# The later steps of the mLSTM gates at later places among the projections' matmuls, and the masked factors as a step of their own

## The chip, the cores and the metric

The kernel runs on one core of a Trainium2 chip. The metric is the device time of one execution in microseconds (us). The engines of the core are named as in the profile: PE is the matrix engine (PEld its weight loads), DVE the vector engine, ACT the scalar engine with the activation functions, POOL the GpSimd engine, SP the engine that here issues nearly all DMAs (its queue is shown as SPq). Each engine works through its own instructions in order and waits at an instruction until what it needs is there.

## The reference, cut to what matters

One encoder layer over 2048 rows of 1024 columns, in float32. After an RMS norm with conditioning, one input projection gives the columns of a windowed attention and of a bidirectional mLSTM with 4 heads, among them 16 gate columns. The mLSTM needs a depthwise convolution over time of its query and key columns, and from the gates a handful of small vectors per chunk of 128 rows:

```python
logf = blocks(jax.nn.log_sigmoid(f_pre))
bcum = jnp.cumsum(logf, axis=-1)
a = b_last[..., None] - bcum + ig
a_max = jnp.max(a, axis=-1)
w = jnp.exp(a - a_max[..., None])
...
m_new = jnp.maximum(bl + m_st, am)      # scan over the 16 chunks
decay = jnp.exp(bl + m_st - m_new)
...
m_t = jnp.maximum(g, jnp.max(dlog, axis=-1))
dw = jnp.exp(dlog - m_t[..., None])
inter = jnp.exp(g - m_t)
```

This is done for 4 heads, 2 directions and 16 chunks, 128 rows of 128 numbers in all. Then follow the chunks' products, the attention, an output projection and a SwiGLU feed-forward part with 2816 columns.

## The kernel before, in words

Float32 products are made from three matmuls of rounded halves (high by high, high by low, low by high), each of 128x128 weights and 512 columns. The order of the work is written out by hand on PE throughout. In the stretch that matters here it is written out for DVE, ACT, POOL and SP as well (`manual_schedule`): each engine's program order is the order in which the Python code issues its instructions. In some other parts (the end of the first part, the attention part, the end of the feed-forward part) a planner orders the engines other than PE.

The stretch is the loop over 252 steps `i` that starts the projections of the mLSTM's keys and queries. In each step it calls `pull(1)`, which issues one more matmul of the projection now being filled in (`proj_mm`, line 497) and then `beat()`, which counts down the entries of a list of postponed actions (`put_soon`) and runs those that are due. Before the matmul of step `i`, two generators are run on: `gates()` (the gates' arithmetic) and `w_out_ops()` (products of the output projection's weights with a gate row, and their sums, on POOL, with their DMAs on SP). A `yield 62` in one of them means: what follows is issued in step 62, ahead of the matmul of that step.

```python
for i in range(2 * 96 + 60):
    for j, g in enumerate(steps):
        while due[j] <= i:
            due[j] = next(g)
    ...
    pull(1)
```

A projection tile of 128 columns has four blocks of 512 rows, 24 matmuls each (`conv_tile`): block 0 takes steps 0 to 23, block 1 steps 24 to 47, and so on; the next tile starts at step 96, the third at 192. The blocks' sums stand in two PSUM banks in turn, so the matmuls of a block wait until the block before the last one has been read out. In the step after a block's last matmul, ACT takes the middle tap out of the bank (line 524) and the two edge columns (525, then 527 and 528). Seven beats later DVE adds the two outer taps, also out of the bank (`sides`, lines 511 and 512). Then tanh on ACT, a product on DVE and a store to `qk_d` on SP follow one after another for the block before (`finish`; all three are shown as line 121). For the first tile this gives, on DVE: sides of block 0 at the end of step 30, of block 1 at 54, of block 2 at 78, of block 3 at 102; the products of blocks 0 to 3 at the ends of steps 61, 85, 109 and 115; the tanhs on ACT at 57, 81, 105 and 111; the stores on SP at 66, 90, 114 and 120.

`gates()` goes through these parts: the log-sigmoid and its running sums (up to line 869), constants for picking rows (871 to 874), at step 52 the running maximum and the last column of each chunk (`st`, 881 and 882), then a small matmul (885, `rps`) that brings the chunks' values into rows, the scan over the chunks on DVE (887 to 892, `sr`, `mn`, `rw`), an exp (894), the masked factors `rx` (897), four small matmuls that bring the results back to columns (899 and 900, `cps`: the first pair from `rw`, the second from `rx`), their use (`mc`, `dec`, `ux`: 903 to 909), three exps and three products (911 to 917), four stores of rows to `bc_d` on SP (920, 921), three transposes on PE (924) and their copies (926). The mLSTM reads these results from step 252 on; its first scan (over the chunks backwards) transposes key blocks (611, `ktp`) that come back from `qk_d` by DMA (588, `mqk`).

`w_out_ops()` works through eight units. Unit n has its POOL products and sums (957, 959, 970) at steps 33, 36 and 41 plus 24n, its stores (972, 973) at 49 + 24n and (962) at 62 + 24n, and issues the loads of unit n + 1 (935) at 41 + 24n; units 4 to 7 stand 10 steps further back.

Of the kernel before, what the change touches and what calls it, by code (L numbers as in the profile page):

```python
# [36 lines left out]
def hybrid_layer_kernel(  # L37
# [14 lines left out]
    def bank(tag, name):  # L52
        return pp.tile([P, 512], F32, tag=tag, name=name, bufs={"g": 2, "a": 2, "b": 1, "c": 2, "d": 1}[tag])
# [782 lines left out]
    def gates():  # L836
# [43 lines left out]
        for sl, j in ((lo_, 127), (hi_, 0)):  # L880
            dve.tensor_scalar(st[sl, 0], spot[sl], b[sl, j:j + 1], None, MUL)
            dve.scalar_tensor_tensor(st[sl, 1], spot[sl], cm[sl, j:j + 1], st[sl, 0], MUL, ADD)
        yield 62
        ps = bank("c", "rps")
        pe.matmul(ps[:8, :2 * NT], pick, st.rearrange("p j c -> p (j c)"), start=True, stop=True)
        sr = s2.tile([8, 2, NT], F32, name="sr", bufs=1)
# [3 lines left out]
        dve.tensor_copy(rw[:, 0, 1:], mn[:, :-1])  # L890
        dve.tensor_tensor(rw[:, 1], sr[:, 0], mn, SUB)
        dve.tensor_tensor(rw[:, 2], rw[:, 1], rw[:, 0], ADD)
        yield 76
        act.activation(rw[:, 2], rw[:, 2], AF.Exp)
        yield 84
        rx = s2.tile([8, 8, NT], F32, name="rx", bufs=1)
        dve.tensor_tensor(rx, rowm, rw[:, 2].unsqueeze(1).to_broadcast([8, 8, NT]), MUL)
        ps = bank("c", "cps")
        pe.matmul(ps[:, :2 * NT], rowm.rearrange("q r c -> q (r c)"), rw[:, :2].rearrange("q j c -> q (j c)"), start=True, stop=True)
        pe.matmul(ps[:, P:2 * P], ones[:8, :], rx.rearrange("q r c -> q (r c)"), start=True, stop=True)  # L900
# [6 lines left out]
        act.activation(q4(dec[:, 64:])[:, :, ::-1], q4(ps[:, P + 64:2 * P]), AF.Copy)  # L907
        ux, it, em, wr = gt("gux"), gt("git"), gt("gem"), gt("gwr")
        dve.tensor_scalar(ux, cm, mc[:, 0:1], None, MAX)
        yield 92  # L910
        act.activation(it, ux, AF.Exp, bias=mc[:, 0:1], scale=-1.0)
        act.activation(wr, r, AF.Exp, bias=mc[:, 1:2])
        dve.tensor_tensor(em, b, ux, ADD)
        yield 100
        act.activation(em, em, AF.Exp, scale=-1.0)
        dve.tensor_scalar(it, it, float(128 ** -0.5), None, MUL)
        dve.tensor_scalar(ux, ux, -1.0, None, MUL)
        yield 112
        for d, sl in ((0, lo_), (1, hi_)):
            sp.dma_start(bc_d[:, :, d, :].rearrange("h c t -> (h c) t"), ux[sl])  # L920
            sp.dma_start(bc_d[:, :, 2 + d, :].rearrange("h c t -> (h c) t"), it[sl])
# [58 lines left out]
    w_second = proj_cols(C_QM)  # L980
    win = ExitStack()
    steps = [gates(), w_out_ops()]
    due = [0, next(steps[1])]
    win.enter_context(tc.manual_schedule(engines={getattr(mybir.EngineType, e) for e in ("DVE", "Activation", "Pool", "SP")}))
# [1024 lines left out]
```

## Time and profile before

| | us |
|---|---|
| median of 3 runs | 2263.84 (2262.03 to 2265.5) |
| the profiled execution, its own time | 2262.92 |
| span of the profile (first to last instruction) | 2261.1 |
| PE busy in the span | 2219.7 (98%) |
| DVE busy | 1611.6 (71%) |
| ACT busy | 1061.4 (47%) |
| POOL busy | 1041.5 (46%) |

The gates' stretch runs from 175.4 us (the first transposes of the gates) to 238.4 us (the first transpose of the mLSTM). Times in the rows of the timeline are microseconds from the start of the span; a row's second number is its duration, a bracket at its end says how long the engine stood idle before it and who ended that.

### The profile page before, as it was taken

Reading aid. Unit: us, or ns where it says so; the run is one execution under the profiler, and the core shown is the slowest. Engines: PE = TensorE matmul, PEld = TensorE weight load, DVE = VectorE, ACT = ScalarE, POOL = GpSimd, SP = SyncE. Lnnn points to the kernel's source line nnn. Section 1 sums busy time; section 2 is a strip of 40 time slices with the busy share of each in tenths; the row PEclk is TensorE's granted clock in tenths of the full one; section 3 lists DMA queues with packets and bytes.
Section 4 is the critical chain, followed back from the end, with each engine's and each line's share of the span. In section 5 each row is a group of like instructions: output and inputs, shape, how many; then the busy total and the mean of one; then the engine's idle time right before and its main releaser. Section 6 shows DMA issues by size and latency. Waiting matters only on the chain.

```text
span 2261.1 us, 32357 instructions
## 1 busy us (share of the span) xinstructions
PE 2219.7 (98%) x10818; PEld 1858.9 (82%) x10818; DVE 1611.6 (71%) x2942; ACT 1061.4 (47%) x2209; POOL 1041.5 (46%) x904
## 2 busy tenths in 40 slices
PE   7999999999999999999999999999999999999998
PEld 4997888888788878888888888888888888888887
DVE  6776667656688887886667777777766665785694
ACT  5433665554678746354445444433333333233452
POOL 1016535334344333436666565467665663692020
PEclk8999999999999999999999999999999999999999
DMA  8566755685766576764343455534333374543462
GB/s 323 169 208 200 227 166 170 190 241 168 209 185 189 175 242 209 266 234 156 107 144 110 153 182 170 170 126 140 98 112 98 112 260 141 172 149 95 145 217 93
DMA packets 337063, 391.28 MB, mean 173 GB/s; under 512 B 20874, under 2 KB 234234, under 8 KB 336896
## 3 DMA queue, kind: packets, MB, share of 16 engines
q1 hardware_dynamic: 335616, 388.65, 52.8%
q8 instruction: 85, 1.39, 0.3%
q14 instruction: 82, 0.67, 0.1%
q10 hardware_dynamic: 1280, 0.56, 0.1%
HBM read 269.95 MB, written 119.19 MB: 172 GB/s over the span
## 4 chain that ended last, share of the span: by engine, by line
PE 88%; DVE 5%; ACT 2%; DMA 2%; issue 1%; POOL 1%; SPq 0%; POOLq 0%; ACTq 0%; DVEq 0%
PE gps L497 15%; PE fp L56 12%; PE fp L57 12%; PE fp L58 12%; PE fo L58 5%; PE fo L57 5%; PE fo L56 5%; PE ops L56 2%; PE ops L58 2%; PE ops L57 2%; PE atp L807 1%; PE num L708 1%; PE kvp L621 1%; PE num L710 1%; PE pv L56 1%
## 5 line engine op out<-in xcount | busy, mean ns | idle before, releaser
L497 PE MATMUL gps<-hT,whi 128*128 128x512 f32 x1088 | 395.1, 418 | 0.0
L58 PE MATMUL fo<-w,al 128*128 128x512 f32 x616 | 239.8, 389 | 0.0
L56 PE MATMUL fo<-w,ah 128*128 128x512 f32 x616 | 239.7, 389 | 0.0
L57 PE MATMUL fo<-w,ah 128*128 128x512 f32 x616 | 239.7, 389 | 0.0
L497 PE MATMUL gps<-hT,wlo 128*128 128x512 f32 x544 | 226.1, 416 | 0.0
L497 PEld LDWEIGHTS gps<-hT,whi 128*128 128x128 f32 x1088 | 199.5, 189 | 23.5
L56 PE MATMUL fp<-T,S 128*128 128x512 f32 x528 | 206.7, 391 | 0.3 <-ACT s L1622 0.3
L57 PE MATMUL fp<-T,S 128*128 128x512 f32 x528 | 205.7, 389 | 0.0
L58 PE MATMUL fp<-T,S 128*128 128x512 f32 x528 | 205.4, 389 | 0.0
L1763 DVE TENSOR_TENSOR al<-al,ah 128x1024 fp32r<-128x1024 f32 x77 | 115.0, 1499 | 106.9 <-ACT ah L1762 106.7
L1762 ACT ACTIVATE ah<-al 128x1024 fp32r<-128x1024 f32 x77 | 81.7, 1060 | 181.5 <-DMA al<-a_d 175.9
L1465 DVE TENSOR_TENSOR S<-sf,S 128x512 fp32r<-128x512 f32 x86 | 126.9, 1513 | 37.1 <-ACT S L1464 36.9
L1465 DVE TENSOR_TENSOR A<-graw,A 128x512 fp32r<-128x512 f32 x86 | 128.9, 1518 | 16.7 <-ACT A L1464 16.6
L58 PE MATMUL fp<-B,A 128*128 128x512 f32 x352 | 136.9, 389 | 0.0
L56 PE MATMUL fp<-B,A 128*128 128x512 f32 x352 | 136.9, 389 | 0.0
L57 PE MATMUL fp<-B,A 128*128 128x512 f32 x352 | 136.9, 389 | 0.0
L58 PEld LDWEIGHTS fo<-w,al 128*128 128x128 f32 x616 | 115.6, 188 | 24.6 <-DVE al L1763 0.5
L56 PEld LDWEIGHTS fo<-w,ah 128*128 128x128 f32 x616 | 115.6, 188 | 24.1
L57 PEld LDWEIGHTS fo<-w,ah 128*128 128x128 f32 x616 | 115.6, 188 | 24.1
L800 POOL TENSOR_SCALAR ap<-ap,adn 128x384 f32<-128x384 f32 (+1 forms) x124 | 70.2, 585 | 132.2 <-PE atp L807 62.2
L1469 POOL TENSOR_TENSOR sf<-A,A22r 128x512 f32<-128x512 f32 x42 | 59.3, 1412 | 151.0 <-DMA A22r<-in_w_ffn_in_dram 134.5
L1632 DVE SCALAR_TENSOR_TENSOR g<-t,g 128x512 f32<-128x512 f32 x44 | 42.1, 957 | 114.0 <-ACT t L1631 114.0
(440 smaller groups left out, 6156.9 us busy)
## 6 DMA issues: line engine op xcount, KB each, us to landing
al<-a_d SPq DMA_DIRECT2D x77, 512.0 KB, 4.2
wmod<-in_w_mod_dram SPq DMA_DIRECT2D x48, 512.0 KB, 7.4
graw<-in_w_ffn_in_dram SPq DMA_DIRECT2D x43, 512.0 KB, 3.8
a_d<-ka SPq DMA_DIRECT2D x66, 256.0 KB, 4.9
bc<-bc_d SPq DMA_DIRECT2D x64, 256.0 KB, 4.8
hop_d<-n SPq DMA_DIRECT2D x56, 256.0 KB, 4.1
a_d<-u SPq DMA_DIRECT2D x55, 256.0 KB, 4.6
mqk<-qk_d SPq DMA_DIRECT2D x44, 256.0 KB, 4.5
```

Source lines behind the costliest of these rows:

```text
L56: pe.matmul(o, lh, rh, start=first, stop=False, skip_group_check=skip)
L57: pe.matmul(o, lh, rl, start=False, stop=False, skip_group_check=skip)
L58: pe.matmul(o, ll, rh, start=False, stop=last, skip_group_check=skip)
L497: pe.matmul(ps, w[i == 2][:, k, :], hT[n](i == 1, k), start=(k == 0 and i == 0), stop=(k == KT - 1 and i == 2))
L621: pe.matmul(kvp[:, :129], kn, vw, start=True, stop=True)
L708: pe.matmul(num[:, d, :129], sc[:, d, :], va_c, start=True, stop=st is None)
L800: pool.tensor_scalar(p, p, dn[:, g:g + 1], 0.0, MUL, ADD)
L1465: dve.tensor_tensor(t[:, 1, :], f, t[:, 0, :].bitcast(F32), SUB)
L1469: add.tensor_tensor(f1, a21, a22, ADD)
L1632: dve.scalar_tensor_tensor(g0, t0, 1.0, g0, ADD, MUL)
L1762: act.activation(ah, al.bitcast(F32), AF.Copy)
L1763: dve.tensor_tensor(al, al.bitcast(F32), ah.bitcast(F32), SUB)
```

## The change

Only the step numbers in `gates()` change, from the small matmul `rps` on, and one `yield` is added between the masked factors `rx` and the matmuls `cps`. What stood at step 62 (`rps` and the scan) stands at 74, the exp goes from 76 to 86, `rx` from 84 to 92, `cps` and what uses it from 84 to 102, the exps from 92 to 110 and from 100 to 118, the stores, transposes and copies from 112 to 130.

```diff
             dve.scalar_tensor_tensor(st[sl, 1], spot[sl], cm[sl, j:j + 1], st[sl, 0], MUL, ADD)
-        yield 62
+        yield 74
         ps = bank("c", "rps")
         pe.matmul(ps[:8, :2 * NT], pick, st.rearrange("p j c -> p (j c)"), start=True, stop=True)
...
         dve.tensor_tensor(rw[:, 2], rw[:, 1], rw[:, 0], ADD)
-        yield 76
+        yield 86
         act.activation(rw[:, 2], rw[:, 2], AF.Exp)
-        yield 84
+        yield 92
         rx = s2.tile([8, 8, NT], F32, name="rx", bufs=1)
         dve.tensor_tensor(rx, rowm, rw[:, 2].unsqueeze(1).to_broadcast([8, 8, NT]), MUL)
+        yield 102
         ps = bank("c", "cps")
         pe.matmul(ps[:, :2 * NT], rowm.rearrange("q r c -> q (r c)"), rw[:, :2].rearrange("q j c -> q (j c)"), start=True, stop=True)
         pe.matmul(ps[:, P:2 * P], ones[:8, :], rx.rearrange("q r c -> q (r c)"), start=True, stop=True)
...
         dve.tensor_scalar(ux, cm, mc[:, 0:1], None, MAX)
-        yield 92
+        yield 110
         act.activation(it, ux, AF.Exp, bias=mc[:, 0:1], scale=-1.0)
         act.activation(wr, r, AF.Exp, bias=mc[:, 1:2])
         dve.tensor_tensor(em, b, ux, ADD)
-        yield 100
+        yield 118
         act.activation(em, em, AF.Exp, scale=-1.0)
         dve.tensor_scalar(it, it, float(128 ** -0.5), None, MUL)
         dve.tensor_scalar(ux, ux, -1.0, None, MUL)
-        yield 112
+        yield 130
         for d, sl in ((0, lo_), (1, hi_)):
             sp.dma_start(bc_d[:, :, d, :].rearrange("h c t -> (h c) t"), ux[sl])
             sp.dma_start(bc_d[:, :, 2 + d, :].rearrange("h c t -> (h c) t"), it[sl])
```

## The prediction

> **What bounds the kernel now.** I read the page's busy times first, then PE's waits between 140 and 280 us, then the stretch's table and the timelines of PE, DVE, POOL, ACT and SP around the moved steps.
>
> ```profile
> PE 2219.7 (98%) x10818; PEld 1858.9 (82%) x10818; DVE 1611.6 (71%) x2942; ACT 1061.4 (47%) x2209; POOL 1041.5 (46%) x904
> PE cps L900 <- DVE rx L897: 2.1, 1, 2.1
> PE rps L885 <- DVE st L882: 1.7, 1, 1.7
> 190.00:200.00 10.00, 6.40 (x29) 4.91 (x30) 9.04 (x14) 2.44 (x7) 9.84 (x12) 1.00 0.77 242
> 206.80 31.77 PE gps L497 x140
> ```
>
> PE is the bound of the kernel. Between 140 and 280 us it waits twice only, at the two small gate matmuls that the change moves. In the table's row for 190 to 200 us PE works 6.40 of 10 us, DVE 9.04 and POOL 9.84, at a granted clock of 1.00: here the vector engine sets the pace. The last row, of the chain of work, gives the price of one step: 31.77 / 140 = 0.227 us.
>
> ```profile
> 189.24 0.61 PE L497 MATMUL gps<-hT,whi 128*128 128x512 f32 x2
> 191.52 0.23 PE L885 MATMUL rps<-st,pick 128*8 128x32 f32 x2 [1.66 <-DVE st L882]
> 191.68 0.50 PE L497 MATMUL gps<-hT,wlo 128*128 128x512 f32 x1
> 192.02 0.64 PE L497 MATMUL gps<-hT,whi 128*128 128x512 f32 x2
> 196.93 0.40 PE L899 MATMUL cps<-rw,rowm 8*128 8x32 f32 x2
> 199.41 0.48 PE L900 MATMUL cps<-rx,ones_r 8*128 8x128 f32 x2 [2.08 <-DVE rx L897]
> 199.82 0.73 PE L497 MATMUL gps<-hT,whi 128*128 128x512 f32 x2
> 241.62 0.27 PE L611 MATMUL ktp<-ident,mqk 128*128 128x128 f32 x1
> ```
>
> The matmuls at 189.24 are those of steps 60 and 61. Step 62 was due at 189.24 + 2 x 0.227 = 189.69, and `rps` started at 191.52: 1.83 us lost. The second pair of `cps` was due one pair after 196.93 (the `rps` pair took 191.68 - 191.52 = 0.16), at 197.09 to 197.33 if the pair's whole 0.40 is counted, and started at 199.41: 2.1 to 2.3 us lost, I take 2.2. Together 4.03 us, 0.18% of the time. This is all that the change can save.
>
> **The change part by part.** Nothing is added or removed but one place to stop; only positions move. What counts is which work stands ahead of which on each queue, and what is late next.
>
> ```profile
> 190.28 1.19 DVE L882 SCALAR_TENSOR_TENSOR st<-spot,gates,st 64x16 f32<-64x16 f32 x1
> 191.50 0.75 DVE L511 SCALAR_TENSOR_TENSOR cacc<-gps,cvw,cacc 128x511 f32<-128x511 f32 x1
> 192.35 0.75 DVE L512 SCALAR_TENSOR_TENSOR cacc<-gps,cvw,cacc 128x511 f32<-128x511 f32 x1
> 193.02 1.04 DVE L121 SCALAR_TENSOR_TENSOR cacc<-ctanh,cacc 128x512 f32<-128x512 f32 x1
> 193.98 0.17 DVE L887 COPY sr<-rps 8x32 f32<-8x32 f32 x1
> 194.74 1.19 DVE L890 COPY rw<-mn 8x15 f32<-8x15 f32 x1
> 195.85 0.15 DVE L891 TENSOR_TENSOR rw<-sr,mn 8x16 f32<-8x16 f32 x1
> 196.04 1.15 DVE L892 TENSOR_TENSOR rw<-rw 8x16 f32<-8x16 f32 x1
> 197.95 0.75 DVE L512 SCALAR_TENSOR_TENSOR cacc<-gps,cvw,cacc 128x511 f32<-128x511 f32 x1
> 198.62 0.73 DVE L897 TENSOR_TENSOR rx<-rowm,rw 8x128 f32<-8x128 f32 x1
> 200.15 1.23 DVE L909 TENSOR_SCALAR gates<-gates,mc 128x128 f32<-128x128 f32 x1
> 201.30 1.80 DVE L121 SCALAR_TENSOR_TENSOR cacc<-ctanh,cacc 128x512 f32<-128x512 f32 x1
> ```
>
> *`rps`, 62 to 74.* `st` is there at 191.47 as before, since nothing ahead of it moves; PE follows a DVE result after 0.05 us (191.47 to 191.52). Without the old wait PE runs on to step 72, due at 189.24 + 12 x 0.227 = 191.96. There block 3 of the tile takes the bank of block 1, and DVE reads that bank (lines 511 and 512, queued behind `st`) until 193.10. So PE stops at step 72 until 193.15: **a new wait of 1.19 us**. Before, PE came to step 72 only at 192.02 + 9 x 0.227 = 194.06, and the bank was free. `rps` at step 74 then starts at 193.15 + 0.45 = 193.60 and is through by 193.9. DVE is busy with line 121 until 194.06, so `sr` starts at its old time and the scan ends as before, at 197.19. The side sums of block 2 (issued at step 78 in both versions) end at 198.70 as before.
>
> *Step 96, a second bank.* `rps` and its restart cost 192.02 - 191.52 - 0.227 = 0.27. Step 96 (next tile, bank of block 2) is due at 193.60 + 0.27 + 22 x 0.227 = 198.86; DVE frees the bank at 198.70. No wait, with 0.1 us to spare; a miss of a few tenths here would cost as much.
>
> *The exp, 76 to 86, and the exps after it.* They now stand behind other tanhs. The three rows of ACT show what that costs:
>
> ```profile
> 188.28 1.28 ACT L121 ACT_TABLE_LOAD   x1
> 197.22 0.21 ACT L894 ACTIVATE rw<-rw 8x16 f32<-8x16 f32 x1 [1.37 <-DVE rw L892]
> 197.34 0.61 ACT L121 ACTIVATE ctanh<-cacc 128x512 f32<-128x512 f32 x1
> ```
>
> The first tanh (step 57) brought its table at 188.28; exp at 197.22 and tanh at 197.34 follow each other with no load between. All moved exps stand behind step 57 in both versions: no load is added, cost 0. The exp still starts at about 197.2, when the scan is done, and tanh of block 1, now ahead of it, has finished by then.
>
> *`rx`, 84 to 92, and `cps`, 84 to 102.* Here the order on DVE turns over: the product of block 1 (line 121, step 85) now stands **ahead of `rx`** instead of behind `ux`. POOL decides what it costs.
>
> ```profile
> 192.76 1.90 POOL L970 TENSOR_TENSOR ts<-by,ts 128x256 f32<-128x256 f32 x2
> 194.62 1.28 POOL L957 TENSOR_TENSOR bx<-bx,gb 128x512 f32<-128x512 f32 x1
> 195.86 1.30 POOL L959 TENSOR_TENSOR by<-by,gb 128x512 f32<-128x512 f32 x1
> 198.50 1.52 POOL L970 TENSOR_TENSOR ts<-by,ts 128x256 f32<-128x256 f32 x2
> ```
>
> The 8x15 copy `rw` took 1.19 us and ended at 195.93, just after POOL's product (194.62 + 1.28 = 195.90); `rw` at 196.04 ended with POOL's next one; between two POOL instructions the same kind took 0.15. I therefore let each such DVE instruction end behind the POOL instruction that it meets. The product of block 1 starts behind 198.70, meets the first sum of the row at 198.50 (half of 1.52) and takes 1.04 us like its twin at 193.02, to about 199.8; `rx` then meets the second sum and takes 0.73, to 200.55. PE sees it at 200.60. The first pair of `cps` is due at 198.86 + 6 x 0.227 = 200.22, the second at 200.38: **a wait of 0.2 us**. Bounds: with DVE undisturbed (the product for what is left of 1.80 when POOL's 1.30 is taken off, and 0.15), `rx` is ready at 199.4 and the wait is 0. With the dearest rows (1.80 and 1.23) it is ready at 201.73 and the wait 1.4. I take 0.2 since the POOL row that it meets is known.
>
> The Trainium skill (SBUF — State Buffer, § Who interferes with whom) says that of a GpSimd instruction and a VectorE one that needs the shared pair of ports, the later waits for the whole of the other, and that this does not hold for VectorE instructions with one SBUF input and no two-port mode. The trace agrees: lines 511 and 512, which read PSUM, stay at 0.75 us while POOL works. This speaks against the change, for it lets `rx` meet a second POOL instruction; by the rule the saving is the sum below, and without it 0.2 us more.
>
> *Steps 110 to 130.* After `rx` the rest of DVE's work up to step 130 is the same as before in another order. The bank of block 3, wanted at step 120, is read out behind `mc` and `ux` (1.23): `cps` restarts PE at about 201.0, DVE ends the side sums at 201.2 + 1.23 + 1.6 = 204.0, step 120 comes at 201.1 + 18 x 0.227 = 205.2: no wait, 1.2 us to spare. If that cover is gone it costs PE that much less the margin. The transposes at step 130 need `em`, whose exp comes some 2 us earlier on ACT; step 252 reads the copies 27 us later. Cost 0.
>
> *The four stores to `bc_d`, 112 to 130, on SP.*
>
> ```profile
> 203.13 0.34 SPq L121 DMA_DIRECT2D qk_d<-cacc  x1
> 206.32 0.51 SPq L920 DMA_DIRECT2D bc_d<-gates  x1
> 208.31 0.60 SPq L921 DMA_DIRECT2D bc_d<-gates  x1
> 208.95 0.60 SPq L935 DMA_DIRECT2D bx<-in_w_out_dram  x1
> 230.02 0.63 SPq L972 DMA_DIRECT2D wo_d<-bx  x1
> 235.83 0.33 SPq L588 DMA_DIRECT2D mqk<-qk_d  x1
> ```
>
> They are moved past the loads of unit 4 (935, step 113), the stores of blocks 2 and 3 (114, 120) and those of unit 3 (121), which all go 208.95 - 206.32 = 2.6 us earlier in the queue, and they now stand in front of the stores at 144 and the loads at 147. The queue also stops less: the store of block 1 waited for its product until 203.13; that product now ends at 199.8. So SP is some 3 us early at step 113 and, with DVE done with step 118 at about 207.5, about 3 us early again behind the four stores. POOL gets unit 4 earlier by as much. Cost 0, as long as that holds (a rival below).
>
> **The sum.** 4.03 - 1.19 - 0.2 = **2.6 us saved**; with the bounds of the second wait 1.4 to 2.8, and 4.0 if no wait comes in place of the old ones. Behind step 252 PE is the bound and everything is queued in the same order, so the shift should last. Against the profiled execution (2262.92, span 2261.1) that is 2260.3. The median of the runs is 0.92 above that execution, so I forecast 2263.84 - 2.6 = **2261.2 us**, 0.12% less. What a measurement of this kernel can tell from no change is about 0.2%, 4.5 us: so the forecast is "within".
>
> **The rivals.**
>
> *A. The wait only changes its name.* DVE is 90% busy from 190 to 200 us, and none of its work goes away. If it meets POOL as dearly as in the worst rows, `rx` is late by 1.4 us, and step 120 takes another 0.5 to 1: saved 4.03 - 1.19 - 1.4 - 0.8 = 0.6, time 2263.2. For it: the row at 201.30 (1.80). Against: POOL's rows do not move before 200 us, and they give 0.2.
>
> *B. All of it is saved.* If bank 1 is free by step 72, or PE waits there for something that I misread, 4.0 us go: 2259.8. Against: line 512 ends at 193.10, 1.1 us behind step 72's new time.
>
> *C. Slower: SP brings the second key block late.* The transpose at 241.62 needs the block whose load went out at 235.83; that load waited for the store at 230.02, which waited for SP and POOL. The page's median from issue to landing is
>
> ```profile
> mqk<-qk_d SPq DMA_DIRECT2D x44, 256.0 KB, 4.5
> ```
>
> so it landed at about 240.3, 1.3 us ahead of its use. PE now comes at 239.0. If SP does not move up with PE, PE waits 1.3; if the four stores, 2.6 us of SP, wait for DVE and hold up the stores at 144 and the loads at 147 by their full length, the block lands at 242.9 and PE waits 3.9: net 1.3 us slower, 2265.1. It decides in PE's favour of the old kernel from 3.9 us of wait minus 2.6 saved, that is when SP is more than 1.3 us later than before at that load. Against: step 118 would have to end behind 211 us, and I get 207.5.
>
> The Trainium skill (DMA: Bandwidth & Descriptors, § Issuing engines are not separate DMA queues) calls the sequencer's time for starting a DMA usually small beside the DMA itself. The rows here have 0.51 to 0.60 us for one start beside 4.5 to landing, and four starts in a row make 2.6 us. By the page rival C would cost next to nothing and the sum would stand; by the rows it has the price above.
>
> *D. Slower elsewhere.* The planner orders the other engines in the attention part anew from shifted times:
>
> ```profile
> 720.00:830.00 110.00, 104.39 (x538) 86.20 (x537) 93.39 (x218) 76.17 (x170) 41.02 (x57) 1.00 0.67 211
> ```
>
> PE idles 5.6 us there. An order worse by as much gives 2261.2 + 5.6 = 2266.8; an order better by half gives 2258.4. Nothing in the profile speaks for either.
>
> **How the numbers follow.** Forecast 0.50, A 0.14, B 0.10, C 0.12, D 0.14 (two in three of it slower). The forecast alone has 2260.0 to 2263.0; the runs before spread by 1.8 to either side of their middle. The range goes from 2258.4 (D's better side) to 2266.8 (its worse side). Faster by over 0.2% (below 2259.3) takes a third of B, the better part of D and a little of the forecast: 0.12. Slower by over 0.2% (above 2268.4) takes what of C and D goes beyond its price: 0.16. Within: 0.72.
>
> **What the profile after would show.** `rps` and the second pair of `cps` without the waits of 1.7 and 2.1; a wait of about 1.2 us of a `gps` matmul for line 512, right before `rps`; `rx` behind line 121 on DVE, ending near 200.6, and PE at `cps` waiting a few tenths; the first key transpose of the mLSTM at about 235.8 instead of 238.4; the `bc_d` stores behind the stores of unit 3. The forecast is wrong if step 72 does not wait, if step 96 or 120 waits by over half a us, if the key transposes wait for `mqk`, or if the shift at 238 us is gone or has grown by the end.

## The result and the profile after

The changed kernel has a median of 2260.43 us over 14 runs (2257.48 to 2263.07). The kernel before, run beside it, has 2264.14 over 14 runs (2262.03 to 2269.16). The ratio is 0.9983 with a 95% interval of 0.9976 to 0.9990: faster by 3.7 us (the interval reaches from 2.3 to 5.4 us), less than the 0.2% named in the prediction, but the interval excludes 1. The forecast was 2261.2 us, 2.6 us less. The profiled execution took 2260.36 us, its span is 2258.6 us. Behind line 897 the changed kernel's lines, and those of the experiments made from it, have numbers higher by one: `cps` is 900 and 901, `bc_d` 921 and 922. In the kernel with the sides first they are higher by one from line 881 on already, and by two behind 897.

Of the changed kernel, the first fence has the page's busy times, the second PE's waits between 140 and 240 us, the third the table's row for 190 to 200 us (its columns: length, then the busy time of PE, PEld, DVE, ACT and POOL, the granted clock, the DMA share, GB/s).

```profile
PE 2219.7 (98%) x10818; PEld 1859.0 (82%) x10818; DVE 1608.5 (71%) x2942; ACT 1061.3 (47%) x2209; POOL 1043.7 (46%) x904
```

```profile
PE gps L497 <- DVE cacc L512: 0.9, 1, 0.9
```

```profile
190.00:200.00 10.00, 9.14 (x42) 6.73 (x40) 9.26 (x13) 3.74 (x10) 9.84 (x12) 1.00 0.72 231
```

The two waits of before (`rps` for `st` and `cps` for `rx`) are gone. One wait is left, at another place: a projection matmul for the bank that line 512 reads. In the ten microseconds from 190 us PE now works 9.14 instead of 6.40 us; DVE and POOL are as full as before. The timelines of PE and of DVE around the moved steps:

```profile
191.04 0.39 PE L497 MATMUL gps<-hT,wlo 128*128 128x512 f32 x1
192.29 0.73 PE L497 MATMUL gps<-hT,whi 128*128 128x512 f32 x2 [0.86 <-DVE cacc L512]
192.95 0.23 PE L885 MATMUL rps<-st,pick 128*8 128x32 f32 x2
...
199.69 0.40 PE L900 MATMUL cps<-rw,rowm 8*128 8x32 f32 x2
199.94 0.46 PE L901 MATMUL cps<-rx,ones_r 8*128 8x128 f32 x2
...
234.84 0.27 PE L611 MATMUL ktp<-ident,mqk 128*128 128x128 f32 x1
```

```profile
189.38 1.21 DVE L882 SCALAR_TENSOR_TENSOR st<-spot,gates,st 64x16 f32<-64x16 f32 x1
...
191.48 0.75 DVE L512 SCALAR_TENSOR_TENSOR cacc<-gps,cvw,cacc 128x511 f32<-128x511 f32 x1
...
197.74 1.17 DVE L121 SCALAR_TENSOR_TENSOR cacc<-ctanh,cacc 128x512 f32<-128x512 f32 x1
198.83 0.82 DVE L897 TENSOR_TENSOR rx<-rowm,rw 8x128 f32<-8x128 f32 x1
...
201.71 0.75 DVE L512 SCALAR_TENSOR_TENSOR cacc<-gps,cvw,cacc 128x511 f32<-128x511 f32 x1
```

Step 72 was due at 191.04 + 0.227 = 191.27 us. It started at 192.29, just behind line 512 (191.48 + 0.75 = 192.23). `rx` ended at 199.65, and PE came to the pair that needs it at 199.94 without a wait.

To compare runs I use one length: from the first transpose of the gates (line 841, at 175.38 us before and 174.68 after) to the first key transpose of the mLSTM (line 611, 238.41 and 234.84). Before it is 63.03 us, after 60.16: **2.87 us gained in the stretch**. The mLSTM's last key transposes start at 499.1 us before and 494.7 after: there PE is 4.4 us early. At the end of the span it is 2261.1 - 2258.6 = 2.5 us. The runs below show where some of it went.

### The profile page after: what moved, and what is told of

Its sections match the earlier page's. It is cut to its first block, busy times and chain, and to the rows that moved or that the text cites. A ratio compares the mean times of both kernels' runs of the same rounds, so it can differ in the third digit from the quotient of the medians.

```text
span 2258.6 us, 32358 instructions
## 1 busy us (share of the span) xinstructions
PE 2219.7 (98%) x10818; PEld 1859.0 (82%) x10818; DVE 1608.5 (71%) x2942; ACT 1061.3 (47%) x2209; POOL 1043.7 (46%) x904
## 3 DMA queue, kind: packets, MB, share of 16 engines
q8 instruction: 85, 1.39, 0.3%
## 4 chain that ended last, share of the span: by engine, by line
PE 88%; DVE 5%; DMA 3%; ACT 3%; issue 1%; SPq 1%; POOL 0%; ACTq 0%; POOLq 0%; DVEq 0%
PE gps L497 14%; PE fp L56 12%; PE fp L57 12%; PE fp L58 12%; PE fo L58 5%; PE fo L56 5%; PE fo L57 5%; PE ops L56 2%; PE ops L58 2%; PE ops L57 2%; PE kvp L621 1%; PE num L708 1%; PE atp L807 1%; PE num L710 1%; PE pv L56 1%
## 5 line engine op out<-in xcount | busy, mean ns | idle before, releaser
L800 POOL TENSOR_SCALAR ap<-ap,adn 128x384 f32<-128x384 f32 (+1 forms) x124 | 70.2, 585 | 134.6 <-PE atp L807 62.2
```

The source lines that it names most:

```text
L800: pool.tensor_scalar(p, p, dn[:, g:g + 1], 0.0, MUL, ADD)
```

## The experiments

All intervals in this part are that length. "Waits" are PE's waits in the stretch, "clock" is PE's granted clock from 180 to 215 us.

| kernel | interval, us | waits in the stretch, us | clock |
|---|---|---|---|
| before | 63.03 | `rps` 1.7, `cps` 2.1 | 1.00 |
| before, second profile | 65.80 | `rps` 1.2, `cps` 2.1 | 0.90 |
| after | 60.16 | line 512: 0.9 | 1.00 |
| after, second profile | 60.64 | line 512: 1.4 | 1.00 |
| `rps` alone | 62.62 | line 512: 1.0, `cps` 0.2 and 1.9 | 1.00 |
| `rps` back | 62.51 | `rps` 1.8 | 0.95 |
| stores alone | 63.51 | `rps` 1.2, `cps` 1.4 | 0.95 |
| no POOL work in the stretch | 59.01 | none | 1.00 |
| sides first | 59.01 | none | 1.00 |

### Only `rps` is moved

```diff
 (the kernel before)
-        yield 62
+        yield 74
         ps = bank("c", "rps")
```

> Only the small matmul rps and the scan behind it go from step 62 to 74; everything later stays where it was before the change. Measured by the interval from the first transposes of the gates (line 841) to the first key transpose of the mLSTM (line 611): 238.41 - 175.38 = 63.03 us before the change, 234.84 - 174.68 = 60.16 after it. Theory (PE is held to DVE's queue, and a wait that is taken away comes back at the next thing that DVE owes): the wait of 1.7 us before rps goes, a wait of about 0.9 us for line 512 comes at step 72, and the wait before the second pair of cps at step 84 takes up all the rest, since rx stands at its old place on DVE's queue and ends when it did: interval 63.0 +- 0.3, time as before within 0.1%. Rival (each wait is a cost of its own): 1.83 - 1.0 = 0.8 us less, interval 62.2.

The time is 2263.24 us beside 2263.35 of before; ratio 0.9998 (0.9989 to 1.0007), no difference. The timeline of PE:

```profile
192.25 0.73 PE L497 MATMUL gps<-hT,whi 128*128 128x512 f32 x2 [0.97 <-DVE cacc L512]
192.91 0.23 PE L885 MATMUL rps<-st,pick 128*8 128x32 f32 x2
...
195.81 0.40 PE L899 MATMUL cps<-rw,rowm 8*128 8x32 f32 x2 [0.17 <-DVE rw L891]
198.12 0.48 PE L900 MATMUL cps<-rx,ones_r 8*128 8x128 f32 x2 [1.91 <-DVE rx L897]
```

The wait for `st` becomes a wait for bank 1, and PE, which now comes earlier to `cps`, still waits there for `rx`: 0.97 + 0.17 + 1.91 = 3.05 us of waits in place of 1.66 + 2.08 = 3.74. The interval, 62.62 us, lies just below the expected 62.7 to 63.3, and as far from the rival's 62.2 as from the 63.03 of before. Moving `rps` by itself brings nothing that the times can tell; most of the wait moves on to the next place where DVE is late.

### The changed kernel with `rps` back at step 62

```diff
 (the changed kernel)
-        yield 74
+        yield 62
         ps = bank("c", "rps")
```

> The changed kernel with rps and the scan put back from step 74 to 62; all later steps stay where the change put them. Theory: the wait before rps is back at 1.7 us, no wait at step 72 (PE comes there 2 us later than after the change, when the bank is free), and none before cps at step 102, where rx ends just in time: saved against before 2.2 us, interval 60.8 +- 0.3, time 2262.0 against 2264.1 before. So most of the change's saving belongs to cps. Rival (the move of rps brings what the change brings): the interval stays above 62.

The interval was 62.51 us, and the expected one was missed by 1.7. The cause stands in the timeline and in the table of stretches:

```profile
193.33 0.22 PE L885 MATMUL rps<-st,pick 128*8 128x32 f32 x2 [1.80 <-DVE st L882]
...
194.65 1.05 PE L497 MATMUL gps<-hT,whi 128*128 128x512 f32 x2
```

```profile
193.83:194.30 0.47, 0.47 (x3) 0.38 (x2) 0.36 (x2) 0.00 (x0) 0.47 (x2) 1.00 1.01 320
194.30:197.71 3.41, 3.41 (x10) 2.63 (x9) 3.34 (x6) 0.26 (x1) 3.33 (x5) 0.51 0.36 127
197.71:201.00 3.29, 3.29 (x16) 2.70 (x15) 3.15 (x6) 1.87 (x6) 3.29 (x4) 0.99 1.01 313
```

About one microsecond behind the wait PE's clock was granted at half for 3.41 us, and a pair of matmuls took 1.05 us in place of 0.62. That costs half of 3.41, 1.7 us, on top of the wait. Without it the interval is 60.8 us: with `cps` moved away from `rx` the second wait is gone, and the first one is priced as in before. The time, 2261.66 us, lies between the two kernels; its ratio to before (0.9992, 0.9984 to 1.0001) has an interval that takes in 1.

### Only the stores to `bc_d` are moved

```diff
 (the kernel before)
-        yield 112
+        yield 130
         for d, sl in ((0, lo_), (1, hi_)):
```

> The kernel before the change with only its last part moved: the four stores to bc_d, the three transposes and the copies go from step 112 to 130. Theory: both waits stay, interval 63.0 +- 0.2, time as before within 0.1%, though the loads of unit 4 go out some 2.5 us earlier on SP. Rival (the saving comes from SP's queue, which is free earlier): interval at or below 62, or the same interval and 2 us or more saved later, between 240 and 560 us.

The stretch was no shorter: 63.51 us, 0.3 more than the expected range. The two waits were a little shorter than in before, and the clock dropped right behind the second one (a pair at 1.13 us):

```profile
190.64 0.23 PE L885 MATMUL rps<-st,pick 128*8 128x32 f32 x2 [1.22 <-DVE st L882]
...
197.83 0.48 PE L900 MATMUL cps<-rx,ones_r 8*128 8x128 f32 x2 [1.38 <-DVE rx L897]
198.24 1.13 PE L497 MATMUL gps<-hT,whi 128*128 128x512 f32 x2
```

The time is 2262.9 us, ratio 0.9993 (0.9985 to 1.0002), an interval that takes in 1. Both old waits are there: the place of the stores on SP is not what removes them. Nor is 2 us saved further back: the first product of the attention (line 780) starts at 578.6 us, before at 579.0.

### POOL's work taken out of the stretch

```diff
 (the kernel before, w_out_ops; units 0 to 3 of 8)
-            pool.tensor_tensor(bx, bx, gb[c_], MUL)
+            if n > 3:
+                pool.tensor_tensor(bx, bx, gb[c_], MUL)
...
-            pool.tensor_tensor(by, by, gb[c_], MUL)
+            if n > 3:
+                pool.tensor_tensor(by, by, gb[c_], MUL)
...
-                pool.tensor_tensor(t, f, g, SUB)
+                if n > 3:
+                    pool.tensor_tensor(t, f, g, SUB)
+            if n < 4:
+                ta, tb = bx, by
```

> The kernel before the change, without the products and sums of units 0 to 3 on POOL (lines 957, 959, 970): the weights of those units are stored unmultiplied and the sums are not made, so a part of the output projection's operands is not computed; all steps stay where they were. It asks why DVE is late. Theory (DVE's small instructions each end with the POOL instruction that they meet): without POOL the four instructions that make st take about 0.15 us each instead of 0.55 to 1.23, st is there by 188.6 and rps has no wait; the scan's copies fall from 1.2 to 0.2 us, rx comes before cps is due: both waits go, interval 63.0 - 4.0 = 59.0 +- 0.4. Rival (DVE has too many instructions in this stretch, POOL or not): at least 1.5 us of the two waits stay, interval above 60.5.

This kernel leaves out a part of the output projection's operands and serves for its times alone. No instruction of the gates was moved, and both waits went. The time is 2259.13 us, ratio 0.9976 (0.9965 to 0.9986). Its row of the table for 180 to 215 us, and two rows of DVE's timeline:

```profile
180.00:215.00 35.00, 35.00 (x158) 28.39 (x157) 19.34 (x50) 14.53 (x34) 8.45 (x10) 1.00 0.75 234
```

```profile
186.07 0.23 DVE L882 SCALAR_TENSOR_TENSOR st<-spot,gates,st 64x16 f32<-64x16 f32 x1
...
193.87 0.27 DVE L897 TENSOR_TENSOR rx<-rowm,rw 8x128 f32<-8x128 f32 x1
```

PE is busy 35.00 of 35 us, DVE 19.34. The same row of before:

```profile
180.00:215.00 35.00, 31.26 (x140) 25.14 (x139) 28.61 (x48) 13.02 (x30) 25.65 (x28) 1.00 0.66 206
```

With POOL still, DVE does 50 instructions in 9.3 us less than 48 of before: the second line 882 takes 0.23 us instead of 1.19 in before and 1.21 in after, line 897 0.27 instead of 0.73 and 0.82. DVE is late because its instructions end behind POOL's. And the floor of the stretch is measured: 63.03 - 59.01 = 4.02 us is all that these waits cost in an execution without a drop of the clock.

### Everything further back, and the side sums ahead of `st`

If the wait at step 72 comes from the side sums that queue behind `st`, then it goes when they are issued first, and when the steps stand further back still:

```diff
 (the changed kernel)
         dve.tensor_tensor_scan(cm[hi_, ::-1], zr[hi_, ::-1], r[hi_, ::-1], -3e38, ADD, MAX)
+        yield 55
         st = s2.tile([P, 2, NT], F32, name="st", bufs=1)
...
-        yield 74
+        yield 80
         ps = bank("c", "rps")
...
-        yield 86
+        yield 90
         act.activation(rw[:, 2], rw[:, 2], AF.Exp)
-        yield 92
+        yield 96
         rx = s2.tile([8, 8, NT], F32, name="rx", bufs=1)
...
-        yield 102
+        yield 112
         ps = bank("c", "cps")
...
-        yield 110
+        yield 118
...
-        yield 118
+        yield 127
...
-        yield 130
+        yield 140
```

> The changed kernel, with the column picks that make st (lines 881 and 882) in a step of their own at 55, behind the side sums of block 1, and everything later some steps further back (rps 80, exp 90, rx 96, cps 112, then 118, 127, 140). Theory (PE waits at step 72 because st stands ahead of the side sums that free block 1's bank): the side sums of block 1 end about 3 us earlier, no wait at step 72, none at rps and none at cps: interval from line 841 to line 611 59.1 +- 0.3 us (the change has 60.16), about 1 us less than the change's time. Rival (DVE is simply full, and some bank is late wherever the steps stand): a wait of 0.5 us or more appears at another matmul between 175 and 210 us, and the interval stays above 59.8.

This kernel is the fastest: **2256.36 us** (2255.61 to 2258.15, 5 runs) beside 2265.47 of before in the same session, ratio 0.9960 (0.9947 to 0.9972). Its timeline of DVE and its row of the table:

```profile
188.93 0.75 DVE L512 SCALAR_TENSOR_TENSOR cacc<-gps,cvw,cacc 128x511 f32<-128x511 f32 x1
189.59 1.08 DVE L882 TENSOR_SCALAR st<-spot,gates 64x16 f32<-64x16 f32 x1
```

```profile
180.00:215.00 35.00, 35.00 (x158) 28.37 (x157) 29.99 (x51) 14.22 (x34) 30.37 (x32) 1.00 0.74 235
```

Block 1's bank is read out by 189.68 us, DVE is as slow as ever (29.99 us), and PE is busy 35.00 of 35 us all the same. The interval is 59.01, the floor that the run without POOL gave. So the wait of 0.9 to 1.4 us left in the changed kernel is for this bank, and in this stretch POOL's interference costs nothing once PE is not made to wait for its outcome. The run does not tell whether the later steps had to move as well, for both were changed at once. The medians differ by 9.1 us and the profiled spans by 2261.1 - 2255.6 = 5.5; the stretch explains 4.0 of it, and where the rest comes from is not settled.

### Second profiles of both kernels

> The changed kernel once more, as it is, beside the version above and in a second profile. Theory: interval 60.2 +- 0.2 with one wait of about 0.9 us at step 72 and granted clock 1.00 from 180 to 240 us, since no gap of PE there is longer than 1 us. Rival (the clock falls now and then whatever the gaps): a stretch at half clock between 180 and 240 us.

> The kernel before, in a second profile. The runs with the same two waits (rps put back, stores alone) each had one stretch of 3.4 us at half the granted clock right behind one of the waits, the first profile of the kernel before had none. Theory (a gap of 1.5 us or more brings such a stretch in some executions and not in others): either interval 63.0 +- 0.2 with clock 1.00, or about 1.6 us longer with one stretch of about 0.5 behind line 885 or 900. Rival (it belongs to the edits of those two runs): clock 1.00.

The changed kernel gave 2260.05 us over 8 runs (0.9976, 0.9965 to 0.9986). Its wait at step 72 was longer this time, so the interval of 60.64 us lies above the expected 60.0 to 60.4; the clock stayed at 1.00. The first fence is of the changed kernel's timeline, the others are of the kernel before, PE's timeline and the table's row:

```profile
196.63 0.73 PE L497 MATMUL gps<-hT,whi 128*128 128x512 f32 x2 [1.35 <-DVE cacc L512]
```

```profile
190.66 0.23 PE L885 MATMUL rps<-st,pick 128*8 128x32 f32 x2 [1.24 <-DVE st L882]
...
198.57 0.77 PE L900 MATMUL cps<-rx,ones_r 8*128 8x128 f32 x2 [2.12 <-DVE rx L897]
...
200.71 1.05 PE L497 MATMUL gps<-hT,whi 128*128 128x512 f32 x2
```

```profile
180.00:215.00 35.00, 31.65 (x128) 25.10 (x127) 27.58 (x48) 12.18 (x28) 24.61 (x27) 0.90 0.68 213
```

In this profile of the kernel before the clock fell to half for twice as long, 35.00 x 0.10 = 3.5 us lost where the first profile lost none. So the interval is 2.8 us longer, where the expectation had 1.6 for a single stretch of 3.4 us. The kernel before has these drops in some executions and not in others. In the stretch they came in four of the six profiles of kernels that kept one or both of the old waits (the kernel before twice, `rps` alone, `rps` back, stores alone, and the next kernel, which has the stretch unchanged: 0.95), and in none of the four of kernels without them.

### What a gap on PE does to its clock

To see whether a wait brings the drop, twenty waits of ten lengths were put where PE otherwise never stops, into the feed-forward part of the kernel before. DVE makes one to ten copies, and a small matmul needs the last:

```diff
 (the kernel before, in the feed-forward part, behind the sum g0)
+            nth[0] += 1
+            if 23 < nth[0] < 44:
+                for _ in range(1 + nth[0] % 10):
+                    dve.tensor_copy(cols, ps2[:, :112])
+                pe.matmul(bank("d", "pps")[:8, :32], cols[:, :8], cols[:, 8:40], start=True, stop=True)
```

> The kernel before with twenty waits put into the feed-forward part, where PE otherwise runs through: in pairs 24 to 43, behind the second product, DVE copies 112 columns from its bank 1 to 10 times (the number goes round), and a small matmul on the copy follows on PE. So PE gets gaps of about 1 to 3.5 us, some 19 us apart. It asks from which length a gap makes the clock fall. Theory: a gap shorter than about 1.5 us never does, one of 2 us or more does in about half of the cases or more, each time for one stretch of 3.4 us at 0.5, which costs about 1.7 us on top of the gap. Rival (only a whole window without work does): the Trainium skill (TensorE: Matmul & The Clock Gate, Part 1) puts the fall behind at least one idle window of about 3.4 us; then none of these gaps, or only the longest, brings a fall.

Four of the twenty, and the ten microseconds behind each (the clock is the third number from the end):

```profile
1606.96 0.22 PE L1633 MATMUL pps<-cols 128*8 128x32 f32 x2 [1.42 <-DVE cols L1632]
1628.19 0.22 PE L1633 MATMUL pps<-cols 128*8 128x32 f32 x2 [1.73 <-DVE cols L1632]
1649.71 0.22 PE L1633 MATMUL pps<-cols 128*8 128x32 f32 x2 [2.04 <-DVE cols L1632]
1861.22 0.22 PE L1633 MATMUL pps<-cols 128*8 128x32 f32 x2 [1.73 <-DVE cols L1632]
```

```profile
1606.96:1616.96 10.00, 10.00 (x45) 8.25 (x46) 5.67 (x5) 4.10 (x8) 8.67 (x6) 1.00 0.61 216
1628.19:1638.19 10.00, 10.00 (x45) 8.27 (x46) 4.45 (x5) 4.12 (x8) 4.97 (x4) 1.00 0.23 79
1649.71:1659.71 10.00, 10.00 (x38) 8.07 (x39) 4.53 (x4) 2.75 (x5) 6.66 (x5) 0.83 0.40 148
1861.22:1871.22 10.00, 10.00 (x38) 8.10 (x39) 1.99 (x3) 2.75 (x5) 3.81 (x3) 0.83 0.22 75
```

| gap, us | 1.11 | 1.42 | 1.73 | 2.04 | 2.35 | 2.66 to 3.89 |
|---|---|---|---|---|---|---|
| gaps | 2 | 2 | 2 | 2 | 1 | 11 |
| clock dropped behind | 0 | 0 | 1 | 2 | 1 | 11 |

A clock of 0.83 over 10 us is 3.4 us at half, 1.7 us lost; behind two of the longest gaps (one of 3.58 and one of 3.89 us) the drop lasted twice as long. A gap of 1.4 us costs its own length; one of 2.0 us costs its length and 1.7 us more.

Length is not all: one gap of 1.73 us brought a drop and the other none. The times at which the drops begin tell more. In each profile they lie whole multiples of 3.413 us apart (here 1650.41, 1674.30 and 1862.03 us are among them: 7 and 62 such steps from the first). So the time of a profile falls into windows of 3.413 us, and PE's idle time can be counted in each. The window that holds most of the gap and the one behind it, for the two gaps of 1.73 us:

```profile
1626.52:1629.93 3.41, 1.74 (x9) 1.45 (x10) 2.61 (x5) 0.00 (x0) 0.00 (x0) 1.00 1.05 329
1629.93:1633.34 3.41, 3.41 (x17) 2.83 (x16) 0.80 (x2) 1.64 (x3) 3.13 (x3) 1.00 0.14 55
1858.62:1862.03 3.41, 1.68 (x9) 1.07 (x8) 1.42 (x4) 0.00 (x0) 0.00 (x0) 1.00 1.01 297
1862.03:1865.44 3.41, 3.41 (x10) 2.64 (x9) 0.00 (x0) 0.00 (x0) 2.30 (x2) 0.50 0.41 152
```

The first gap is cut by the border at 1626.52 us, and 3.41 - 1.74 = 1.67 us of it lie in one window; the second lies in one window whole. Counted between 100 and 2230 us of all ten profiles: all 30 windows at full clock with 1.73 us of idle PE or more were followed by one at half clock, and of the 32 with 0.8 to 1.68 us only one was (stores alone, at 194.96 us: 1.38 us idle, with the small `cps` matmuls in the same window).

The old waits of the gates, 1.2 to 2.1 us, lie at this edge, and the windows lie differently in each execution. The wait of 2.08 us before `cps` (197.33 to 199.41 us) was cut by a border at 198.08 in the first profile of before, into 0.75 and 1.33 us, and no drop followed. The one of 2.12 us in the second lay in one window, 195.21 to 198.62 us. The first row is of the first profile, the others are of the second:

```profile
198.08:201.49 3.41, 2.08 (x9) 1.70 (x10) 2.83 (x8) 0.41 (x3) 3.33 (x5) 1.00 0.64 184
```

```profile
195.21:198.62 3.41, 1.29 (x7) 0.75 (x6) 3.19 (x4) 0.73 (x2) 3.33 (x5) 1.00 1.02 319
198.62:205.45 6.83, 6.83 (x17) 5.25 (x18) 4.93 (x9) 1.69 (x5) 6.33 (x7) 0.50 0.43 134
```

## Why the prediction was right, point by point

**All that can be saved, 4.03 us.** Right: 4.02 us, by the kernels that have no wait left (59.01 against 63.03).

**`rps`: a new wait of 1.19 us at step 72.** Right in place and cause: PE's only wait in the stretch is at that matmul, for line 512. By the due time it lost 192.29 - 191.27 = 1.02 us, and 1.5 in the second profile. DVE's own time varies against PE's from run to run: it came to `st` 0.90 us earlier than in before, PE to its step 0.69 us earlier. What I had not priced is that the first pair behind the stop takes longer: `rps` follows it after 192.95 - 192.29 = 0.66 us, not 0.45.

**`cps`: a wait of 0.2 us.** The term was over-sized: none in either profile. `rx` was ready at 199.65. `st` shows DVE 0.90 us ahead of its old times, so that is 200.55 by them, the predicted 200.55. The way there (line 121 ahead of `rx`, each ending behind a POOL instruction) was as told. What was off is PE's way: step 72 ties it to DVE, and from there to the second pair it took 199.94 - 192.29 = 7.65 us where the working had 200.38 - 193.15 = 7.23. Half of the difference is the slower first pair behind the stop, most of the rest the starts of the two small pairs. So PE came 0.3 us behind `rx`, and that it needed no wait is luck of a few tenths, not a faster DVE. Together the new waits cost 60.16 - 59.01 = 1.15 us where I had 1.39.

**POOL's hold on DVE.** The prediction let `rx` meet a second POOL instruction and counted 0.2 us for it. The run without POOL's work shows how large the effect is from 180 to 215 us: 9.3 us of DVE's time.

**Steps 96 and 120, the tables, the gates' transposes.** No wait at any of them, and no table load beside the moved exp (at 196.34 us on ACT). Block 3's bank was read out by 202.46, before step 120.

**The four stores and rival C.** SP issued them behind unit 3's stores and was early everywhere, as predicted. The rows of SP's queue, of the changed kernel:

```profile
202.12 0.56 SPq L936 DMA_DIRECT2D bx<-in_w_out_dram  x1
...
206.71 0.51 SPq L921 DMA_DIRECT2D bc_d<-gates  x1
...
209.22 0.60 SPq L922 DMA_DIRECT2D bc_d<-gates  x1
...
230.18 0.33 SPq L588 DMA_DIRECT2D mqk<-qk_d  x1
```

Unit 4's load is 6.8 us earlier than before (208.95), the second key block 5.65 us (235.83), and PE only 3.57. Rival C is refuted for this change. It is not far off: in the run without POOL's work PE came to the first key transpose 1.5 us earlier still (233.31 us), and at 241.36 it waited 0.43 us for a key block.

**Rivals A, B and D.** A, the wait that only changes its name, is for the most part what `rps` alone does; with `cps` moved as well it does not hold. B would need bank 1 to be free at step 72, which, with POOL at work, it is only with the side sums ahead of `st`. D did not happen: outside the moved steps the traces have the instructions of DVE, ACT, POOL and SP in the order of before. The step of its own for `rx` should change nothing by itself, for no other instruction of DVE stands between steps 92 and 102; that was not run. The chance of 0.16 for a time above 2268.4 us had no price behind it: the worse times given for C and D, 2265.1 and 2266.8, both lie below.

**"The shift should last."** Only in part. The lead was 579.0 - 574.6 = 4.4 us at the first product of the attention (line 780) and 776.4 - 774.3 = 2.1 us at the last one. PE's wait for a load there, of before and then of after, and after's row of the table for 580 to 610 us:

```profile
PE as L780 <- DMA ak<-kst_d: 1.1, 1, 1.1
```

```profile
PE as L780 <- DMA ak<-kst_d: 2.0, 1, 2.0
```

```profile
580.00:610.00 30.00, 26.88 (x136) 22.44 (x137) 21.10 (x64) 21.55 (x58) 12.82 (x22) 0.94 0.59 173
```

PE, now earlier, waits 0.9 us longer for the same load, and the clock falls behind it: 30.00 x 0.06 = 1.8 us, where before has 1.00. The second profile of the changed kernel has 1.5 us and 0.94. The kernel with the sides first has 1.0 us and no drop although it comes as early. The load took 5.99 us from issue to use in after, 5.12 in before; why it lands later there is not settled.

**The sum and the medians.** The profiled executions differ by 2262.92 - 2260.36 = 2.56 us, and 2.6 was predicted. That is partly luck: 0.7 us of it is an earlier start of the gates, 2.87 is the stretch, 0.8 came on top by the first product of the attention (0.7 of it a wait for ACT at 338 us that of the two profiles only before's has), 2.3 were given back within the attention, and 0.4 came back by the end. The medians differ by 3.7 us; 2.6 lies in the interval of 2.3 to 5.4. Some of the difference is clock. Each run's mean granted clock is listed to three digits:

| | runs | mean time, us | mean clock | time x (1 - clock), us |
|---|---|---|---|---|
| before (in the sessions of the experiments) | 41 | 2264.0 | 0.99383 | 14.0 |
| after | 22 | 2260.1 | 0.99450 | 12.4 |
| sides first | 5 | 2256.7 | 0.99480 | 11.7 |

Of the 3.9 us between the first two rows 1.5 us (standard error 0.4) is clock; the other 2.4 us is close to the 2.6 of the sum. That split is an estimate, for the rows mix sessions: in the one session with both kernels (12 and 8 runs) the means differ by 4.9 us, 1.3 of it clock. Nor is it shown that the 1.5 us belongs to the gates: in the two profiles of each kernel the drops there cost before 0 and 3.5 us and after nothing, but those behind line 780 cost after 1.8 us both times and before nothing. What the sum left out is plain all the same: it priced the old waits by their length, in an execution whose clock stayed at 1.00, and not by the drop that follows them in other executions. One profiled execution could not show it.

## What to carry to other kernels

When a matmul waits for a slow engine, moving that one matmul back only brings the matrix engine sooner to the next thing that engine owes it: list every later place where it waits for the same queue, and put the work that frees a PSUM bank ahead of work that can wait. A stop of the matrix engine near two microseconds can be dearer than its length, by 1.7 us or more here, so short stops may be worth removing for the clock alone; look at the granted clock in several executions, since one may show none of it. And a lead won early can be lost again at a load further on: look at the waits behind the stretch too.

## What the runs showed of the hardware that was not expected

That so short a stop slows the matrix engine afterwards was not expected: behind all 14 gaps of 2.04 us and more, one of two of 1.73 us and none of four below 1.5 us. Length alone does not decide, for in the stretch of the gates a gap of 2.08 us was once followed by no drop. In these profiles PE's idle time within one window of 3.413 us does: 30 drops behind 30 windows with 1.73 us or more, one behind 32 with 0.8 to 1.68 us. What brought that one (stores alone, 1.38 us) is not shown. It follows that a gap between some 1.7 and 3.4 us may go free or not by where it falls; that all 14 of the longer gaps brought a drop is in part luck. The Trainium skill (TensorE: Matmul & The Clock Gate, § Why this matters for your kernels) asks for no gaps of the matrix engine above some 3 us between matmuls. The page's window of about 3.4 us (§ What's actually happening) agrees with the 3.41 us of the drop seen here; its bound for the gap does not agree with these runs.

The size of POOL's effect on DVE's small instructions was not expected either. With POOL still, the 8x15 copy (line 890) took 0.16 us in place of 1.19; lines 511 and 512, which read PSUM, took 0.75 us in both cases.
